# Where a third sum of weights is split, which columns it lands in, and when sums of weights are built in DRAM, in a one-core fp32 decoder block

## The chip, the cores and the metric

The kernel runs on one core of one Trainium2 chip. The metric is the device time of one execution in microseconds (us). A kernel is given by the median of several executions; one further execution is profiled, and the profile counts its times from the first instruction of that execution.

## What is computed

The reference is one decoder layer in float32 on 512 tokens of width 1024: an attention part (a sparse-attention mixer and an RWKV-7 mixer, merged by gates) and a gated MLP. The change touches the MLP and the building of its weights, and it moves transfers that stand beside the attention.

```python
def conv_ffn(h, w_up, conv_w, conv_b, w_down):        # h 512x1024, w_up 1024x5632, w_down 2816x1024
    u = h @ w_up
    up = jnp.pad(u, ((0, 0), (CONV_WIDTH - 1, 0), (0, 0)))
    c = conv_b + conv_w[0] * up[:, 0:s]
    for j in range(1, CONV_WIDTH):
        c = c + conv_w[j] * up[:, j:j + s]
    val, gate = jnp.split(c, 2, axis=-1)
    return (jax.nn.silu(gate) * val) @ w_down

for l in range(DEPTH):
    h = rmsnorm(x, attn_norm_g[l])
    proj = h @ w_in[l]
    ...
    o_a = nsa_mixer(...)
    o_b = rwkv7_mixer(...)
    merged = jax.nn.sigmoid(gate_a) * (o_a @ w_proj_a[l]) + jax.nn.sigmoid(gate_b) * (o_b @ w_proj_b[l])
    x = x + (merged @ w_out[l]).astype(x.dtype)
    h2 = rmsnorm(x, ffn_norm_g[l])
    x = x + conv_ffn(h2, w_up[l], conv_w[l], conv_b[l], w_down[l]).astype(x.dtype)
```

## The kernel before

**Products.** Every large product is made of three: an fp32 operand is split into a high part (`whi`, made by ScalarE, ACT, at L129) and a low part (`wlo`, the operand minus its high part, made by VectorE, DVE, at L132 or L367, or by GpSimd, POOL, at L367), and TensorE (PE) adds up high by high, low by high and high by low in PSUM. The PSUM tiles are named `ps_mm`, `ps_a` and `ps_b`. A matrix product of 128x512 takes about 0.23 us on PE and one of 128x256 about 0.12 us. The lines L123, L126, L129, L132 and L141 are those of helpers, so most of the work stands under these few lines, and one tells the instructions apart by their tiles.

**Stages.** First come the norm and the input projections (to 180 us), which build the inputs of the RWKV mixer; then the RWKV scan with the gate projections in its gaps (to 298); then the attention (298 to 392), in which scores are biased and their maxima taken by a custom instruction of DVE (L1274, `nm` is the negated maximum), exponentiated by ACT and scaled by DVE (L136, `P<-P,sm`), while the projection of the RWKV result (`ps_mm<-obT,whi`, weights `w_proj_b`) fills PE's gaps. The low parts of those eight weight tiles are subtracted by POOL (`wlo<-raw,whi 128x512`, L367). Then come the merge, the output projection and the second norm (to 470), the up-projection (470 to 694) and the down-projection (694 to 804).

**Up-projection.** The hidden columns are worked off in 22 pairs of a gate and a value column, numbered n. The pairs n = 5 to 20 are "quartered": the 512 tokens are two halves, the 1024 inputs two halves, and a scheme of seven products in place of eight is used (`quartered()`), 12 matmuls of 128x256 for each product. It needs the quarters B11, B12, B21 and B22 of the weights and three sums of them, `wsum3`, `wsum2` and `wsum4`. `QUARTER_TILES` lists which of these come together as one load: "top" (B11 and B12, whose sum POOL makes by a DMA that adds, L329), "third" (`wsum3`), "mid" (`wsum2`, B21) and "low" (`wsum4`, B22). "Mid" and "low" land in the rotating buffers `raw`; "top" and "third" land in columns of a tile `right` of 128 partitions by 11 columns of 512, which later holds the MLP's hidden values. `QUARTERED` gives, for each n, the first of the two columns of "top" and the one column of "third". All these loads are issued by `wload()` at L327 on the queue of SyncE (SP), one after the other, and one that has to wait holds up those behind it.

`first_quarters()` is called ahead of the pair and splits "top" and "third" into high and low parts; the split of "third" goes into two of the four buffers `split` (in the profile `s<-right`, 128x512 on ACT and then on DVE), taken in turn by even and odd n. `quartered()` then loads the rest, splits "mid" and "low", and makes the seven products; the fifth of them uses the split of "third" and so sets its buffer free. A scheduler places each instruction on its engine in the order in which its inputs and buffers are free in the scheduler's model, so the place of a line in the code is not the place of its instruction.

The finished hidden columns `right[:, i]` with i below 8 are copied to a DRAM tile `kept` by POOL (L1789), since their space is lent to weights, and fetched back by SP (L1760 for columns 0 to 3, L1790 for 4 to 7).

**Sums of weights in DRAM.** `wsum3`, `wsum2` and `wsum4` are built in DRAM ahead of the up-projection, in 48 pieces of 256 KB. Each piece is a copy issued by SP (L303) and then a DMA issued by POOL that adds the second summand (L300) and that has to wait for the copy. `pace()` hangs the pieces onto the ordinary weight loads, which it counts by `event`: `PACE` says how many pieces the SP queue takes behind a load, and POOL gets their additions at the next load.

**POOL's other work beside the attention.** `replicas()` (L1163 and L1165) copies the values into `Vr` by 16 DMAs and the compressed values into `sq` by 8, all issued by POOL. They stand in POOL's queue with the additions of L300 and the subtractions of L367.

**Down-projection.** It has a scheme of seven products too, with items (j, c, n) in a fixed list. `prepare()` makes ready an item two ahead of the product that PE runs: `difference()` builds a sum or difference of weights (into `raw`, `hA` or the tile `T2`, which the profile shows as `T`), and `parts()` splits it into `whi` and `wlo`. Loads of `w_down` are issued by `load_next()` (L1674). The order on DVE and ACT is that of the code here, not the scheduler's.

Of the kernel before, what the change touches and what calls it, by code (L numbers as in the profile page):

```python
# [32 lines left out]
NFH = NF // 2  # L33
# [50 lines left out]
def hybrid_block(ctx: ExitStack, tc: tile.TileContext, A: dict, out: bass.AP):  # L84
# [128 lines left out]
    def norm_tiles(pool_):  # L213
# [5 lines left out]

    order = [f for i in range(NFH) for f in (i, NFH + i)]  # L220

    QUARTERED = {n: ((0 if n % 2 == 0 else 6 if n < 11 else 2), (4 if n < 9 or 11 < n < 18 else 5 if n < 12 else 7))
                 for n in range(5, 21)}

    def weight_tiles():
        def cols(w, o, kt=KT, eng=v):
# [45 lines left out]

    BASE, SPAN = (3, NFH + 2), 1024
    WSUM = {j: [dp.tile([512, SPAN], F32, name=f"wsum{j}{h}") for h in range(2)] for j in (2, 3, 4)}
    QUARTER_TILES = {"top": ("B11", "B12"), "third": (3,), "mid": (2, "B21"), "low": (4, "B22")}

    def up_quarter(name, o, n):
        r, c = 512 * (name[1] == "2"), DFF * (name[2] == "1") + o
# [13 lines left out]
                    yield WSUM[j][h][r:r + 64], a[r:r + 64], b[r:r + 64]  # L292

    pieces, adding, event = sum_pieces(), [], itertools.count()
    PACE = {**{i: 1 for i in (*range(8, 26), *range(43, 49))}, **{i: 2 for i in range(49, 61)}}

    def pace(load):
        while adding:
# [1277 lines left out]
    def by_quarter(w):  # L1576
        return w.rearrange("p (q k) n -> p q k n", q=2)

    def first_quarters(top, third, mid, low):
        hi, lo = two_quarters()  # L1580
        halves(hi, lo, by_quarter(top))
        y = 2 * (next(turnsq) % 2)
        t3 = [split[y + j][:, :, NFH - 3].rearrange("p q (k n) -> p q k n", k=2) for j in range(2)]
        halves(*t3, by_quarter(third))
        return mid, low, (hi, lo), t3

    def quartered():
        mid, low, (h0, l0), (h3, l3) = ahead.pop(0)
        G, V, W = mmb(), mmb(), pa()[:, 0:256]
        act(V[:, 0:256], kc[:, 0:256], AF.Copy, scale=0.0)  # L1590
        U = hB[:, 256 * (NFH + 3):256 * (NFH + 5)]

        def product(o, hi, lo, j, start=False):
            his, los = ([w[:, k] if len(w.shape) == 3 else w[:, k // 2, k % 2] for k in range(4)] for w in (hi, lo))
            for k in range(4):
                mh, ml = moving(j, k)
                if start and k == 0:
                    te.matmul(o, lhsT=his[k], rhs=mh, start=True, stop=False, skip_group_check=True)
                else:
                    mm_on(o, his[k], mh, False)  # L1600
                mm_on(o, his[k], ml, False)
            for k in range(4):
                mm_on(o, los[k], moving(j, k)[0], False)

        for _ in range(len(QUARTER_TILES) - 1 if loads[0][3] == "quarters" else 1):
            wload()
        h1, l1 = two_quarters()
        with tc.high_priority():
            halves(h1[:, 0], l1[:, 0], mid[:, 0:4])
            halves(h1[:, 1], l1[:, 1], mid[:, 4:8])  # L1610
        product(W, h0[:, 0], l0[:, 0], -1, True)
        act(G[:, 0:256], W)
        product(V[:, 0:256], h0[:, 1], l0[:, 1], 0)
        act(V[:, 256:512], V[:, 0:256])
        h2, l2 = two_quarters()
        halves(h2, l2, by_quarter(low))
        product(W, h1[:, 0], l1[:, 0], 1)
        act(U[:, 0:256], W)
        product(G[:, 0:256], h1[:, 1], l1[:, 1], -2)
        wsplit()  # L1620
        product(W, h3, l3, 2)
        act(G[:, 256:512], W)
        act(U[:, 256:512], W)
        product(V[:, 0:256], h2[:, 1], l2[:, 1], 3)
        product(G[:, 256:512], h2[:, 0], l2[:, 0], -3)
        stt(V, V, -1.0, U, ALU.mult, ALU.subtract)
        return G, V
# [103 lines left out]
    def prepare():  # L1731
        k = len(ready)
        j, c, n = items[k]
        while len(summed) < min(k + 2, len(items)):
            difference()
        ready.append((parts(summed[k], n), operand(j, c, n)))

    def spare_half(c, n):
        halves_of(split[0][:, 0, c:c + n], split[0][:, 1, c:c + n], right[:, c:c + n, 0:256])
# [165 lines left out]
```

## Time and profile before

| | us |
|---|---|
| median of 3 runs | 807.81 |
| lowest and highest | 807.55 and 812.0 |
| the profiled execution, device time | 805.67 |
| its span from first to last instruction | 803.6 |
| PE busy | 790.4 (98%) |
| DVE busy | 635.9 (79%) |
| ACT busy | 485.2 (60%) |
| POOL busy | 122.0 (15%) |
| granted clock of PE | 1.000 |

A row of the timeline gives the start of an instruction in us from the first instruction, its duration, the engine, the line, the operation and its tiles, and in brackets how long the engine had been idle before it and what ended that idle time. The records of PE's matmuls overlap, so a matmul's duration there is longer than its share of PE's time; what a stall costs is read from the idle time in the brackets. A row of the waits gives an engine, the line that waited and the instruction waited for, then the total in us, how many times, and the longest. A row of the windows gives the stretch, its length and the busy time of each engine in it with the number of instructions.

### The profile page before, as it was taken

The page shows a single profiled execution, that of the slowest core. Times are in us where ns is not written, and L with a number is a line of the kernel's source. Part 1 is how long each engine was busy: PE and PEld are TensorE (multiplying, and loading weights), DVE is VectorE, ACT ScalarE, POOL GpSimd, SP SyncE. Part 2 cuts the span into 40 slices and gives each one's busy share as a digit, 9 for nine tenths or more (in the row PEclk, how much of TensorE's full clock was granted, in tenths as well). Part 3 has the DMA queues.
Part 4 walks back from the last instruction along what each step waited for, and adds up shares of the span by engine and source line. Part 5 has one row for each costly group of instructions (what it writes and reads, how often), then busy time and mean ns, then how long its engine had stood idle before and what let it go on. Part 6 is the DMA issues. An engine that isn't in the chain of part 4 may idle for free.

```text
span 803.6 us, 15422 instructions
## 1 busy us (share of the span) xinstructions
PE 790.4 (98%) x5829; PEld 672.5 (84%) x5829; DVE 635.9 (79%) x1227; ACT 485.2 (60%) x1003; POOL 122.0 (15%) x168
## 2 busy tenths in 40 slices
PE   8999999999999998999999999999989999999998
PEld 7777788987777887788788898899989999788886
DVE  6477869993665678889685489989989989998895
ACT  6766654563444567778344365678778778546452
POOL 6211013042000157123100000011101100000010
PEclk9999999999999999999999999999999999999999
DMA  7465557647576587455758333687878775676831
GB/s 240 115 157 144 144 114 178 170 110 202 147 127 150 124 211 168 93 126 122 175 162 275 127 95 116 189 233 212 216 197 225 214 206 167 206 245 213 271 106 53
DMA packets 149495, 135.53 MB, mean 169 GB/s; under 512 B 7862, under 2 KB 126573, under 8 KB 148397
## 3 DMA queue, kind: packets, MB, share of 16 engines
q1 hardware_dynamic: 139152, 110.10, 46.3%
q0 software_dynamic: 9216, 21.97, 15.6%
q10 hardware_dynamic: 1052, 2.48, 0.9%
q8 instruction: 46, 0.75, 0.4%
q14 instruction: 29, 0.23, 0.1%
HBM read 122.20 MB, written 31.65 MB: 191 GB/s over the span
## 4 chain that ended last, share of the span: by engine, by line
PE 86%; DVE 6%; DMA 3%; ACT 3%; issue 1%; POOL 0%; DVEq 0%; ACTq 0%; POOLq 0%; SPq 0%
PE ps_mm L123 51%; PE ps_mm L126 11%; PE ps_a L126 8%; PE ps_a L123 7%; PE ps_b L123 4%; PE ps_b L126 2%; DMA right<-wsum 2%; DVE wlo L132 1%; DMA kept<-right 1%; PE ps_b L1348 1%; ACT whi L129 1%; DVE P L136 1%; DMA pra<-in_rwkv_ln_b_dram 1%; PE ps_mm L1348 1%; DVE s L132 0%
## 5 line engine op out<-in xcount | busy, mean ns | idle before, releaser
L129 ACT ACTIVATE whi<-raw 128x512 fp32r<-128x512 f32 (+2 forms) x134 | 117.7, 891 | 101.0 <-PE ps_mm L123 57.9
L123 PE MATMUL ps_mm<-hh,whi 128*128 128x512 f32 (+1 forms) x368 | 142.9, 392 | 0.3 <-DVE hl L141 0.3
L123 PE MATMUL ps_mm<-hl,whi 128*128 128x512 f32 (+1 forms) x368 | 140.7, 386 | 0.0
L367 DVE TENSOR_TENSOR wlo<-raw,whi 128x1024 fp32r<-128x1024 f32 (+1 forms) x57 | 65.3, 1147 | 38.8 <-PE ps_mm L123 21.4
L123 PE MATMUL ps_mm<-hh,wlo 128*128 128x512 f32 (+1 forms) x368 | 88.8, 380 | 0.0
L123 PEld LDWEIGHTS ps_mm<-hh,whi 128*128 128x128 f32 x368 | 69.2, 188 | 17.1 <-issue 1.0
L123 PEld LDWEIGHTS ps_mm<-hl,whi 128*128 128x128 f32 x368 | 69.3, 188 | 12.9 <-issue 1.0
L123 PEld LDWEIGHTS ps_mm<-hh,wlo 128*128 128x128 f32 x368 | 67.1, 188 | 13.5
L300 POOL DMA_DIRECT2D wsum<-in_w_up_dram x48 | 39.2, 859 | 230.7 <-DMA wsum<-wsum 116.6
L132 DVE TENSOR_TENSOR wlo<-raw,whi 128x512 fp32r<-128x512 f32 (+1 forms) x64 | 58.5, 935 | 11.0 <-ACT whi L129 11.0
L141 DVE SCALAR_TENSOR_TENSOR right<-ps_mm,cw,right 128x511 f32<-128x511 f32 (+1 forms) x64 | 45.4, 741 | 1.2 <-ACT right L129 1.2
L129 ACT ACTIVATE P<-P,nm 128x512 f32<-128x512 f32 (+3 forms) x64 | 35.4, 554 | 13.5 <-DVE nm L1274 13.0
L329 POOL DMA_DIRECT2D right<-right x16 | 13.9, 870 | 188.7 <-DVE right L132 76.4
L126 PE MATMUL ps_mm<-hh,whi 128*128 128x256 f32 x128 | 32.2, 284 | 0.1
L126 PE MATMUL ps_mm<-hl,whi 128*128 128x256 f32 x128 | 32.1, 283 | 0.0
L1274 DVE CUSTOM_DVE_ANT_0 P<-ps_a,AB 128x512 f32<-128x512 f32 (+3 forms) x64 | 29.3, 482 | 1.6 <-PE ps_a L123 1.3
L367 POOL TENSOR_TENSOR wlo<-raw,whi 128x512 fp32r<-128x512 f32 (+3 forms) x13 | 22.1, 1701 | 40.0 <-PE ps_mm L123 22.4
L129 ACT ACTIVATE right<-ps_mm,cw 128x512 f32<-128x512 f32 x32 | 23.9, 769 | 4.2 <-DVE ps_mm L141 3.2
L129 ACT ACTIVATE QK<-ps_mm 128x64 f32<-128x64 f32 (+5 forms) x56 | 14.8, 309 | 17.9 <-PE ps_mm L123 13.7
L126 PEld LDWEIGHTS ps_mm<-hh,whi 128*128 128x128 f32 x128 | 24.6, 192 | 0.3 <-ACT ps_mm L129 0.3
L129 ACT ACTIVATE s<-right 128x512 fp32r<-128x512 f32 (+1 forms) x37 | 20.2, 552 | 7.4 <-DMA right<-wsum 6.7
L126 PEld LDWEIGHTS ps_mm<-hl,whi 128*128 128x128 f32 x128 | 24.6, 192 | 0.0
(489 smaller groups left out, 2118.3 us busy)
## 6 DMA issues: line engine op xcount, KB each, us to landing
raw<-in_w_in_dram SPq DMA_DIRECT2D x38, 512.0 KB, 4.6
wsum<-in_w_up_dram POOLq DMA_DIRECT2D x48, 256.0 KB, 4.6
raw<-in_w_down_dram SPq DMA_DIRECT2D x18, 512.0 KB, 4.1
wsum<-wsum SPq DMA_DIRECT2D x32, 256.0 KB, 4.3
right<-in_w_up_dram SPq DMA_DIRECT2D x32, 256.0 KB, 3.9
raw<-wsum SPq DMA_DIRECT2D x32, 256.0 KB, 3.1
raw<-in_w_up_dram SPq DMA_DIRECT2D x32, 256.0 KB, 3.9
raw<-in_w_up_dram SPq DMA_DIRECT2D x12, 512.0 KB, 4.8
```

The source lines that it names most:

```text
L123: te.matmul(o, lhsT=l, rhs=r, start=start, stop=stop)
L126: te.matmul(o, lhsT=l, rhs=r, start=False, stop=stop, skip_group_check=True)
L129: sc.activation(o, i, f, **kw)
L132: v.tensor_tensor(o, a, b, op=op)
L136: v.tensor_scalar(o, a, s1, None, op0=op0)
L141: v.scalar_tensor_tensor(o, a, s, b, op0=op0, op1=op1)
L300: nc.gpsimd.dma_start(o, x, accum_op=ALU.add)
L329: nc.gpsimd.dma_start(raw[:, 4:8], raw[:, 0:4], accum_op=ALU.add)
L367: low = eng.tensor_tensor(lo, raw, hi.bitcast(F32), op=ALU.subtract)
L1274: maxima.append(v.tensor_tensor_reduce(out=P[:, i], in0=o, in1=BT[:, h, 384 - 128 * qt:512], scale=-1.0, scalar=-NEG, op0=ALU.add, op1=ALU ...
L1348: te.transpose(pt[:, 128 * i:128 * i + 128], P[:, 4 * x + i, 128 * k:128 * k + 128], ident)
```

## The change

Three things are edited.

1. `QUARTER_TILES` lists "third" last. `first_quarters()` splits "top" alone; the split of "third" is written in `quartered()`, behind that of "low", and the load that follows it in the list is asked for there. The columns of "third" are now, for n = 5 to 20, 4, 5, 4, 5, 4, 5, 7, 6, 7, 4, 5, 4, 6, 7, 7, 7 (before: 4 for n = 5 to 8, 5 for 9 to 11, 4 for 12 to 17, 7 for 18 to 20).
2. `PACE` gives a second piece to the loads 11, 14, 17 and 20 and one to 37, 39 and 41; loads 49 to 52 get none (two before), 53 gets one, and 54 to 61 get two. The number of pieces is 48 as before.
3. `prepare()` splits the second item of the down-projection before it builds the difference of the third.

```diff
-    QUARTERED = {n: ((0 if n % 2 == 0 else 6 if n < 11 else 2), (4 if n < 9 or 11 < n < 18 else 5 if n < 12 else 7))
-                 for n in range(5, 21)}
+    QUARTERED = {n: ((0 if n % 2 == 0 else 6 if n < 11 else 2), c)
+                 for n, c in zip(range(5, 21), (4, 5, 4, 5, 4, 5, 7, 6, 7, 4, 5, 4, 6, 7, 7, 7))}
...
-    QUARTER_TILES = {"top": ("B11", "B12"), "third": (3,), "mid": (2, "B21"), "low": (4, "B22")}
+    QUARTER_TILES = {"top": ("B11", "B12"), "mid": (2, "B21"), "low": (4, "B22"), "third": (3,)}
...
-    PACE = {**{i: 1 for i in (*range(8, 26), *range(43, 49))}, **{i: 2 for i in range(49, 61)}}
+    PACE = {**{i: 1 for i in (*range(8, 26), 37, 39, 41, *range(43, 49), 53)}, **{i: 2 for i in (11, 14, 17, 20, *range(54, 62))}}
...
-    def first_quarters(top, third, mid, low):
+    def first_quarters(top, mid, low, third):
         hi, lo = two_quarters()
         halves(hi, lo, by_quarter(top))
-        y = 2 * (next(turnsq) % 2)
-        t3 = [split[y + j][:, :, NFH - 3].rearrange("p q (k n) -> p q k n", k=2) for j in range(2)]
-        halves(*t3, by_quarter(third))
-        return mid, low, (hi, lo), t3
+        return mid, low, third, (hi, lo)
 
     def quartered():
-        mid, low, (h0, l0), (h3, l3) = ahead.pop(0)
+        mid, low, third, (h0, l0) = ahead.pop(0)
...
-        for _ in range(len(QUARTER_TILES) - 1 if loads[0][3] == "quarters" else 1):
+        more = loads[0][3] == "quarters"
+        for _ in range(len(QUARTER_TILES) - 2 if more else 1):
             wload()
...
         halves(h2, l2, by_quarter(low))
+        y = 2 * (next(turnsq) % 2)
+        h3, l3 = (split[y + j][:, :, NFH - 3].rearrange("p q (k n) -> p q k n", k=2) for j in range(2))
+        halves(h3, l3, by_quarter(third))
+        if more:
+            wload()
         product(W, h1[:, 0], l1[:, 0], 1)
...
     def prepare():
         k = len(ready)
         j, c, n = items[k]
-        while len(summed) < min(k + 2, len(items)):
+        while k != 1 and len(summed) < min(k + 2, len(items)):
             difference()
         ready.append((parts(summed[k], n), operand(j, c, n)))
+        if k == 1:
+            difference()
```

How the instructions stand is shown at three places. The order on PE is the same in both kernels, row for row.

**ACT, late in pair n = 10.** The tile `right` here is the loaded sum, and `s_5290<-right 128x2x256` is the split of "third" for pair 12; `ps_mm<-ps_a` and `hB<-ps_a` empty PE's accumulators, and `s_5290<-hB` is work on hidden values. Before:

```order
L129 ACTIVATE s_5289<-hB 128x256
L129 ACTIVATE ps_mm<-ps_a 128x256
L129 ACTIVATE hB<-ps_a 128x256
L129 ACTIVATE s_5290<-hB 128x256
L129 ACTIVATE whi<-raw 128x512 x2
L129 ACTIVATE right<-ps_mm,cw 128x512 x2
L129 ACTIVATE ps_mm<-ps_a 128x256
L129 ACTIVATE s_5290<-right 128x2x256
L129 ACTIVATE whi<-raw 128x1024
```

Of the change:

```order
L129 ACTIVATE s_5289<-hB 128x256
L129 ACTIVATE s_5290<-right 128x2x256
L129 ACTIVATE ps_mm<-ps_a 128x256
L129 ACTIVATE hB<-ps_a 128x256
L129 ACTIVATE s_5290<-hB 128x256
L129 ACTIVATE whi<-raw 128x512 x2
L129 ACTIVATE right<-ps_mm,cw 128x512 x2
L129 ACTIVATE ps_mm<-ps_a 128x256
L129 ACTIVATE whi<-raw 128x1024
```

The split for pair 12 moved up by six rows, from pair 11 into pair 10; that for pair 6 moves up in the same way, and those for most other pairs keep their place, nearly two pairs ahead of their product.

**POOL, at the start of the attention.** `sq` and `Vr` are the copies of values, `wsum` the additions to the sums in DRAM, and the subtractions are those of `w_proj_b`. Before:

```order
L1165 DMA sq<-kc 32x64 x6
L367 TENSOR_TENSOR wlo<-raw,whi 128x512
L1163 DMA Vr<-vt 32x256 x12
L300 DMA wsum_103<-in_w_up_dram 64x1024 x2
L1163 DMA Vr<-vt 32x256
L367 TENSOR_TENSOR wlo<-raw,whi 128x512
L1163 DMA Vr<-vt 32x256 x3
L1165 DMA sq<-kc 32x64 x2
L300 DMA wsum_103<-in_w_up_dram 64x1024 x2
L300 DMA wsum_106<-in_w_up_dram 64x1024 x2
```

Of the change:

```order
L1165 DMA sq<-kc 32x64 x6
L367 TENSOR_TENSOR wlo<-raw,whi 128x512
L1163 DMA Vr<-vt 32x256 x16
L1165 DMA sq<-kc 32x64 x2
L367 TENSOR_TENSOR wlo<-raw,whi 128x512
L300 DMA wsum_103<-in_w_up_dram 64x1024
L367 TENSOR_TENSOR wlo<-raw,whi 128x512
L300 DMA wsum_106<-in_w_up_dram 64x1024 x2
```

The two additions between the copies are gone, and the last three `Vr` copies and two `sq` copies stand ahead of the second subtraction in place of behind it.

**DVE, where the down-projection begins.** `T_7886` is the tile `T2`; the first `wlo<-raw,whi` here is the low part of the second item, `wlo_7907<-T_7886,whi_7906` that of the third. Before:

```order
L132 TENSOR_TENSOR T_7886<-raw 128x1024
L141 SCALAR_TENSOR_TENSOR hA<-ps_mm,cw,hA 128x511
L132 TENSOR_TENSOR s_5291<-hB,s_5291 128x256
L141 SCALAR_TENSOR_TENSOR hA<-ps_mm,cw,hA 128x510
L132 TENSOR_TENSOR wlo<-raw,whi 128x1024
L132 TENSOR_TENSOR right<-hA 128x512
L132 TENSOR_TENSOR wlo_7907<-T_7886,whi_7906 128x1024
```

Of the change:

```order
L132 TENSOR_TENSOR wlo<-raw,whi 128x1024
L141 SCALAR_TENSOR_TENSOR hA<-ps_mm,cw,hA 128x511
L132 TENSOR_TENSOR s_5291<-hB,s_5291 128x256
L141 SCALAR_TENSOR_TENSOR hA<-ps_mm,cw,hA 128x510
L132 TENSOR_TENSOR T_7886<-raw 128x1024
L132 TENSOR_TENSOR right<-hA 128x512
L132 TENSOR_TENSOR hB<-right 128x256
L132 TENSOR_TENSOR hB<-hB,right 128x256
L132 TENSOR_TENSOR wlo_7907<-T_7886,whi_7906 128x1024
```

The low part of the second item and the difference for the third changed places, and the low part of the third item stands two short rows later.

## Prediction

> **What bounds the kernel now.** I read the share of busy time first, then PE's waits, then the timeline round each wait.
>
> ```profile
> PE 790.4 (98%) x5829; PEld 672.5 (84%) x5829; DVE 635.9 (79%) x1227; ACT 485.2 (60%) x1003; POOL 122.0 (15%) x168
> PE ps_a L123 <- DVE nm L1274: 2.3, 1, 2.3
> PE ps_a L126 <- ACT hB L129: 1.8, 2, 1.3
> PE ps_a L126 <- ACT ps_mm L129: 1.3, 1, 1.3
> ...
> PE ps_b L123 <- DVE wlo L132: 0.5, 1, 0.5
> ...
> PE ps_b L424 <- DMA pra<-in_rwkv_ln_b_dram: 0.2, 1, 0.2
> ```
>
> PE is busy for 790.4 of 803.6 us, so it is the bound, and the order of its work does not change. The change can win only what PE waits, 13.2 us in all, and of those rows it touches the surroundings of four: 2.3 (in the attention), 1.8 and 1.3 (up-projection), 0.5 (start of the down-projection). That is 5.9 us, less than 1% of the time. A loss has no such lid: a new wait on any engine ahead of PE would show at once.
>
> Since the records of PE overlap, the idle time in a row is a little less than what is lost: matmuls of 128x256 follow one another by 0.12 us while a record lasts 0.28 (four of them take 0.64 at 583.88, below), and those of 128x512 by some 0.23 with 0.39 (two take 0.61 at 701.35). A stall therefore costs its idle time and 0.16.
>
> **Change 1, "third" and its columns.** The two waits of the up-projection, with what stands ahead of them, on POOL, SP, ACT and PE in turn:
>
> ```profile
> 574.97 0.58 POOL L1789 DMA_DIRECT2D kept<-right  x1 [2.56 <-DVE right L132]
> 578.77 0.37 SPq L327 DMA_DIRECT2D right<-wsum  x1
> 583.12 0.63 ACT L129 ACTIVATE s<-right 128x512 fp32r<-128x512 f32 x1 [1.98 <-DMA right<-wsum]
> 591.30 0.63 ACT L129 ACTIVATE s<-right 128x512 fp32r<-128x512 f32 x1 [2.22 <-DMA right<-wsum]
> 583.88 0.64 PE L126 MATMUL ps_mm<-hh,wlo 128*128 128x256 f32 x4
> 585.84 0.75 PE L126 MATMUL ps_a<-s,s 128*128 128x256 f32 x4 [1.31 <-ACT hB L129]
> 594.64 0.74 PE L126 MATMUL ps_a<-s,whi 128*128 128x256 f32 x4 [1.35 <-ACT ps_mm L129]
> 648.66 0.50 PE L126 MATMUL ps_a<-s,s 128*128 128x256 f32 x2 [0.48 <-ACT hB L129]
> ACT s L129 <- DMA right<-wsum: 6.7, 5, 2.2
> ```
>
> The "third" for pair 12 goes into column 4, whose hidden values POOL has to copy away at 574.97; the load is issued at 578.77; ACT stands before the split from 581.14 to 583.12; the evictions behind it in its queue come late, and PE waits at 585.84. Pair 13 uses column 4 again, must wait for the split of pair 12, and the same follows at 591.30 and 594.64. So these two stalls, 1.31 + 0.16 + 1.35 + 0.16 = 2.98 us, hang on one column.
>
> With the change pair 12 uses column 6 and pair 13 column 7, both free long before. Column 4, copied away at 574.97, serves pair 14 only; the split of that stands after the fifth product of pair 12, so with pairs some 10.4 us apart (16 in 166 us) near 597. What is still late is another column at the same point of its life: column 5 for pair 15 and column 6 for pair 17, two and four pairs further on, loads near 600 and 621. From 578.77 to 583.12 issue, landing and waking of ACT took 4.3, so these can be split from about 604 and 625 on, and the splits stand near 607 and 628. They have some 2.7 us to spare. Pair 18 waits for column 7 in both kernels, and its 0.48 stays. The cost of the split itself, 0.63 on ACT and as much on DVE, is the same work for the same 16 pairs: though it is written behind the split of "low", the scheduler puts it as far ahead of its product as before, so there is nothing to price in the pair itself. For pair 6 it moves ahead of the first quartered pair and may wait for its load there; the dearest such wait so far held ACT for 2.22 and cost PE 1.5, the cheapest cost PE nothing (five waits in the row, three stalls). I take 0, with +1.5 as its other end. On SP "third" now stands behind "mid" and "low", which gives these an earlier place, and the order there is otherwise the same. I put change 1 at −3.0, ends −3.6 (the 0.48 and 0.16 go too) and 0.
>
> **Change 2, the pieces.** The first stall in the list stands in the attention:
>
> ```profile
> 306.57 1.28 DVE L136 TENSOR_SCALAR P<-P,sm 128x512 f32<-128x512 f32 x3
> 311.09 2.67 DVE L136 TENSOR_SCALAR P<-P,sm 128x512 f32<-128x512 f32 x1
> 314.41 0.50 PE L123 MATMUL ps_a<-KH,qst 128*128 128x512 f32 x1 [2.31 <-DVE nm L1274]
> 295.94 1.59 POOL L300 DMA_DIRECT2D wsum<-in_w_up_dram  x2 [6.73 <-DMA wsum<-wsum]
> 296.98 3.58 POOL L1165 DMA_DIRECT2D sq<-kc  x6
> 309.95 1.68 POOL L300 DMA_DIRECT2D wsum<-in_w_up_dram  x2
> 311.03 1.13 POOL L1163 DMA_DIRECT2D Vr<-vt  x1
> 311.58 1.88 POOL L367 TENSOR_TENSOR wlo<-raw,whi 128x512 fp32r<-128x512 f32 x1
> 312.80 2.10 POOL L1163 DMA_DIRECT2D Vr<-vt  x3
> 314.33 1.53 POOL L1165 DMA_DIRECT2D sq<-kc  x2
> 315.31 2.29 POOL L300 DMA_DIRECT2D wsum<-in_w_up_dram  x2
> L1163 POOL DMA_DIRECT2D Vr<-vt x16 | 9.4, 664 | 1.9 <-DMA Vr<-vt 1.2 <-DMA wsum<-in_w_up_dram 0.5 <-issue 0.2
> 372.76 1.30 POOL L367 TENSOR_TENSOR wlo<-raw,whi 128x512 fp32r<-128x512 f32 x1 [1.60 <-PE ps_mm L123]
> 373.02 1.07 DVE L132 TENSOR_TENSOR mx<-mx,gts 128x8 f32<-128x8 f32 x1
> ```
>
> Three scalings take 1.28, one takes 2.67 while a subtraction runs on POOL, and PE waits 2.31 for the maxima behind it. The same is seen at 373.02: a tiny operation (8 columns) lasts 1.07, to the end of POOL's 372.76 + 1.30. So it is the subtraction on POOL that stops DVE, not the additions, and the price is what is left of it. The change takes away the additions and so shifts when the subtraction starts. From 311.58 go the two additions at 295.94 (1.04 until the next row) and the two at 309.95 (1.08); ahead of it now come three `Vr` (312.80 to 314.33, 1.53) and two `sq` (to 315.31, 0.98): 311.97. If none of the 1.9 that the `Vr` copies waited comes back, 310.1. A start at 310.1 with 1.88 ends at 311.98, some 0.5 beyond the scaling's usual end of 311.52, and so costs about 0.6; a start at 311.5 costs the 2.3 again; from 311.6 on the scaling has passed. Averaged over the span that is some 1.1 lost of 2.47, so −1.4, ends −2.47 (missed) and 0 (met in full).
>
> The Trainium skill speaks against a row of copies issued by POOL: its page "SBUF — State Buffer", section "A bandwidth-pool intuition that's wrong (but worth ruling out)", has such a DMA at some 620 ns alone and 3100 ns beside a DVE copy. The row of six `sq` above went out 0.60 apart beside a busy DVE, so this case's trace does not bear it out. By the page even one such delay would, as an estimate, put the subtraction past 311.6 and make the term −2.47, if no other scaling is met.
>
> The pieces moved forward go where PE does not wait:
>
> ```profile
> 57.00:130.00 73.00, 73.00 (x462) 57.34 (x461) 57.46 (x78) 42.76 (x64) 12.92 (x14) 1.00 0.58 134
> 222.00:250.00 28.00, 28.00 (x348) 22.36 (x340) 16.44 (x47) 12.41 (x31) 1.59 (x2) 1.00 0.73 136
> ACT whi L129 <- PE ps_mm L123: 19.4, 7, 2.9
> 239.43 0.53 SPq L303 DMA_DIRECT2D wsum<-wsum  x1
> ```
>
> In both stretches PE is busy throughout (73.00 of 73.00, 28.00 of 28.00), and from 57 to 130 ACT waits 19.4 us for PE to set its split buffers free, not for loads. Seven more issues of 0.53 on SP are hidden behind that: 0. With the cover gone they would cost 7 x 0.53 = 3.7. The additions that go with them stand ahead of POOL's `KH` and `KL` copies; POOL is busy 1.59 of 28.00 in the second of these stretches, so I take 0 there too.
>
> **Change 3, the second low part first.**
>
> ```profile
> 694.42 1.23 DVE L132 TENSOR_TENSOR T<-raw 128x1024 f32<-128x1024 f32 x1 [0.95 <-PE ps_mm L123]
> 697.22 1.22 DVE L132 TENSOR_TENSOR wlo<-raw,whi 128x1024 fp32r<-128x1024 f32 x1
> 698.49 0.73 PE L123 MATMUL ps_b<-wlo,s 128*128 128x512 f32 x2 [0.47 <-DVE wlo L132]
> 701.35 0.61 PE L123 MATMUL ps_mm<-wlo,s 128*128 128x512 f32 x2
> 702.57 1.22 DVE L132 TENSOR_TENSOR wlo<-hA,whi 128x1024 fp32r<-128x1024 f32 x1
> 704.07 0.61 PE L123 MATMUL ps_a<-wlo,s 128*128 128x512 f32 x2
> 704.00:800.00 96.00, 95.95 (x429) 79.35 (x428) 81.40 (x93) 47.05 (x60) 2.23 (x4) 1.00 0.54 179
> ```
>
> The low part moves from 697.22 to 694.42 (`T` waited there for PE's last products of the up-projection, and they read the buffer of this low part too), so the 0.47 + 0.16 = 0.63 goes. The difference `T` moves to 697.22 and ends at 698.45; ACT takes 1.06 to split it (699.5), DVE 1.22 for its low part (700.8). PE wants that 0.63 earlier than 701.35, at 700.72: 0.1 late. Behind it on DVE three operations of 0.33, a sum and the next low part (1.13 each) end near 704.1, wanted at 704.07 − 0.63 + 0.1 = 703.5: 0.6 late. What is won is given back within two items, since DVE is full there: 0, ends −0.6 and +0.3. The fetch of the kept columns moves up by one load on SP; from 704 on PE is busy for 95.95 of 96.00, which hides it.
>
> **Sum.** −3.0 − 1.4 + 0 = −4.4. The profiled execution, 805.67 (span 803.6), would become 801.3. It lies 2.1 below the median, and I move the median by the same amount: 807.81 − 4.4 = **803.4 us**.
>
> **Rivals.** *The collision stays whole*: the subtraction starts near 311, for which the working of 311.97 speaks as well as against it; only −3.0 is left, 804.8. *It is missed whole*: −3.0 − 2.5, 802.3. *The wait only moves* to columns 5 and 6 (pairs 15 and 17), because their loads stand behind others on SP and the 2.7 us to spare are used up; for it speaks the traffic there, against it that the split stands later than the load by more than the 4.3 seen; the 3.0 comes back, 806.4. *Slower*: POOL's eight subtractions, all shifted in time, meet DVE's chain more often. Three of eight stretched an operation so far and one reached PE; each full hit costs 2.47. One more in addition to the present one leaves 0.5 of the gain; from two more it decides: 807.81 − 3.0 + 4.9 = 809.7. Against it: after the third subtraction their starts are set by PE setting buffers free, which does not move.
>
> **How the numbers follow.** Chances: the forecast 0.42, collision whole 0.20, missed 0.12, wait moves 0.13, slower 0.09, none of these 0.04. All ends at their best give −3.6 − 2.5 − 0.6 = −6.7, 801.1, and I allow some 0.7 below for the scatter of the runs; upward the range takes in the wait that moves and stops short of no change: 800.4 to 807.6. A measurement can tell about 1% (8.1 us) from no change. Faster by that would take more than all the stalls touched: 0.03. Slower by that would take three further full hits: 0.03. Within 1%: 0.94.
>
> **What would show it.** Right: ACT's waits for "third" fall from 6.7 in five to under 2; no stall of PE of over 1 us between 570 and 600; the stall before L1274's maxima is below 2.3; PE's wait for `wlo` at 698 is gone and smaller ones appear by 704. Wrong: stalls of PE near 608 or 628 (the wait moved); several scalings over 1.5 us (more hits); a wait of PE for a DMA beyond the 0.2 listed, in the first 250 us (the pieces).

## The result, and the profile after

The changed kernel takes 802.39 us (median of 5, 801.76 to 804.24), the kernel before 807.81; the ratio is 0.9934, with a 95% interval of 0.9911 to 0.9958. Forecast were 803.4 us, 800.4 to 807.6, and no change of over 1%.

The waits of PE in the profile after (engine, line and what it waited for, then us in total, times, longest):

```profile
PE ps_b L123 <- issue: 1.8, 1, 1.8
PE ps_b L123 <- DVE warm L156: 1.2, 1, 1.2
PE ps_a L126 <- ACT hB L129: 0.7, 1, 0.7
PE ps_mm L123 <- DVE oaT L132: 0.5, 1, 0.5
PE ps_mm L123 <- DVE wlo L132: 0.4, 1, 0.4
...
PE ps_a L123 <- DVE wlo L132: 0.3, 1, 0.3
```

The wait of 2.3 for DVE's maxima and the two of 1.3 in the up-projection are gone. In place of the 0.5 at the start of the down-projection stand two, 0.4 and 0.3. New is the first row, 1.8 with no cause that the profile shows. The profiled execution happens to be the longest of the five, 804.24 us (span 802.2); what it holds and the others do not is told below.

**Up-projection.** The split of "third" on ACT from pair 12 on, the loads of columns 5 and 6 on SP, and PE's one stall:

```profile
576.40 0.62 ACT L129 ACTIVATE s<-right 128x512 fp32r<-128x512 f32 x1
586.57 0.61 ACT L129 ACTIVATE s<-right 128x512 fp32r<-128x512 f32 x1
...
606.73 0.61 ACT L129 ACTIVATE s<-right 128x512 fp32r<-128x512 f32 x1
...
626.89 0.62 ACT L129 ACTIVATE s<-right 128x512 fp32r<-128x512 f32 x1
643.93 0.63 ACT L129 ACTIVATE s<-right 128x512 fp32r<-128x512 f32 x1 [1.40 <-DMA right<-wsum]
599.93 0.92 SPq L327 DMA_DIRECT2D right<-wsum  x2
621.26 0.37 SPq L327 DMA_DIRECT2D right<-wsum  x1
```

and, of the waits between 517 and 683, the one that had been 6.7:

```profile
ACT s L129 <- DMA right<-wsum: 1.4, 1, 1.4
```

ACT no longer stands before a split until pair 18; its waits for "third" fell from 6.7 us in five to 1.4 in one.

**Attention.** POOL's queue and DVE's scaling:

```profile
295.60 2.97 POOL L1165 DMA_DIRECT2D sq<-kc  x6 [7.44 <-PE ps_b L123]
298.59 1.30 POOL L367 TENSOR_TENSOR wlo<-raw,whi 128x512 fp32r<-128x512 f32 x1
299.82 8.14 POOL L1163 DMA_DIRECT2D Vr<-vt  x16
307.96 0.99 POOL L1165 DMA_DIRECT2D sq<-kc  x2
308.96 1.28 POOL L367 TENSOR_TENSOR wlo<-raw,whi 128x512 fp32r<-128x512 f32 x1
...
311.11 0.49 DVE L136 TENSOR_SCALAR P<-P,sm 128x512 f32<-128x512 f32 x1
```

The 16 copies go out without a gap, the subtraction ends at 310.24, and the scaling begins at 311.11 and takes 0.49 in place of 2.67.

**Down-projection.** DVE's operations that matter, and PE:

```profile
692.48 1.23 DVE L132 TENSOR_TENSOR wlo<-raw,whi 128x1024 fp32r<-128x1024 f32 x1 [1.02 <-PE ps_mm L123]
695.27 1.21 DVE L132 TENSOR_TENSOR T<-raw 128x1024 f32<-128x1024 f32 x1
...
697.58 0.42 DVE L132 TENSOR_TENSOR hB<-hB,right 128x256 f32<-128x256 f32 x1
697.92 1.22 DVE L132 TENSOR_TENSOR wlo<-T,whi 128x1024 fp32r<-128x1024 f32 x1
...
701.20 1.22 DVE L132 TENSOR_TENSOR wlo<-hA,whi 128x1024 fp32r<-128x1024 f32 x1
695.83 0.61 PE L123 MATMUL ps_b<-wlo,s 128*128 128x512 f32 x2
699.20 0.74 PE L123 MATMUL ps_mm<-wlo,s 128*128 128x512 f32 x2 [0.35 <-DVE wlo L132]
702.47 0.74 PE L123 MATMUL ps_a<-wlo,s 128*128 128x512 f32 x2 [0.25 <-DVE wlo L132]
```

PE does not wait at 695.83, where it waited 0.47 before, and does so at 699.20 and 702.47.

**Where the time went.** PE does the same matmuls in the same order in all these kernels, so the nth of one profile can be set beside the nth of another, and the steps in the difference of their starts tell place by place what was won and lost. Against the profile of before (us):

| kernel | attention, at 314 | small matmuls, 385 to 400 | up-projection, 517 to 660 | down-projection, 694 to 745 | elsewhere | all |
|---|---|---|---|---|---|---|
| the change | −2.2 | +3.4 | −3.3 | +0.6 | 0.0 | −1.4 |
| the change again (e12_change_again) | −2.2 | +0.5 | −3.7 | +0.6 | 0.0 | −4.7 |

In its first profile the change wins 4.9 us at the places it touches and loses 3.4 between 385 and 400 to a pause of PE and a slower clock behind it, which the profile of before lacks altogether. In its second the pause costs 0.5.

### The profile page after: what moved, and what is told of

Same layout as the page of the kernel before. It is cut to its first block, busy times and chain, and to the rows that moved or that the text cites. A ratio compares the mean times of both kernels' runs of the same rounds, so it can differ in the third digit from the quotient of the medians.

```text
span 802.2 us, 15423 instructions
## 1 busy us (share of the span) xinstructions
PE 792.6 (99%) x5829; PEld 674.2 (84%) x5829; DVE 633.8 (79%) x1227; ACT 484.2 (60%) x1003; POOL 121.5 (15%) x168
## 4 chain that ended last, share of the span: by engine, by line
PE 90%; DVE 4%; DMA 2%; ACT 2%; issue 1%; POOL 0%; DVEq 0%; POOLq 0%; ACTq 0%; SPq 0%
PE ps_mm L123 51%; PE ps_mm L126 13%; PE ps_a L126 9%; PE ps_a L123 7%; PE ps_b L123 4%; PE ps_b L126 2%; DVE wlo L132 1%; PE ps_b L1348 1%; DMA pra<-in_rwkv_ln_b_dram 1%; PE ps_mm L1348 1%; ACT whi L129 1%; DVE P L1274 0%; DMA kept<-right 0%; DMA right<-wsum 0%; POOL pra L170 0%
## 5 line engine op out<-in xcount | busy, mean ns | idle before, releaser
L1274 DVE CUSTOM_DVE_ANT_0 P<-ps_a,AB 128x512 f32<-128x512 f32 (+3 forms) x64 | 29.3, 481 | 1.8 <-PE ps_a L123 1.5
L129 ACT ACTIVATE whi<-T 128x1024 fp32r<-128x1024 f32 (+1 forms) x12 | 11.9, 991 | 17.7 <-DVE T L132 10.0
```

The costliest lines, as they stand in the source:

```text
L129: sc.activation(o, i, f, **kw)
L1274: maxima.append(v.tensor_tensor_reduce(out=P[:, i], in0=o, in1=BT[:, h, 384 - 128 * qt:512], scale=-1.0, scalar=-NEG, op0=ALU.add, op1=ALU ...
```

## The experiments

Each kernel has one profile; those of more than one run are timed beside the kernel before. The last columns are the steps as above.

| kernel | median us | ratio to before, 95% | attention | 385 to 400 | up-projection | down-projection | all |
|---|---|---|---|---|---|---|---|
| e1_third | 803.44 | 0.9957, 0.9938 to 0.9977 | −0.5 | +1.5 | −3.1 | 0.0 | −2.2 |
| e2_pieces | 805.93 | 0.9981, 0.9962 to 1.0 | −2.2 | +0.9 | −0.8 | 0.0 | −2.1 |
| e3_low_first | 807.54 | 1.0008, 0.9988 to 1.0029 | −1.5 | +3.1 | −0.4 | +0.6 | +1.7 |
| e4_without_low | 801.15 | 0.9923, 0.9898 to 0.9948 | −2.2 | +0.8 | −3.2 | 0.0 | −4.7 |
| e5_columns | 804.26 | 0.9955, 0.9932 to 0.9978 | −1.0 | +1.0 | −3.8 | 0.0 | −3.9 |
| e6_c18_6 | 800.9 | 0.9925, 0.9899 to 0.9952 | −2.2 | +0.5 | −4.3 | 0.0 | −6.0 |
| e7_halves | 804.33 (one run) | | −1.1 | +0.1 | −0.8 | 0.0 | −1.4 |
| e8_pieces_early | 803.43 | 0.9958, 0.9938 to 0.9979 | −2.2 | +0.2 | −3.4 | 0.0 | −1.9 |
| e9_clear | 803.45 | 0.9934, 0.9916 to 0.9951 | −2.2 | 0.0 | −4.3 | 0.0 | −2.2 |
| e10_traffic | 802.85 (one run) | | −2.2 | +0.2 | −4.3 | 0.0 | −2.8 |
| e11_sub_dve | 804.08 (one run) | | −2.2 | +0.2 | −0.9 | 0.0 | −1.3 |
| e12_change_again | 802.46 | 0.9929, 0.9911 to 0.9946 | −2.2 | +0.5 | −3.7 | +0.6 | −4.7 |

The median of the kernel before was 806.85 beside the first four, 808.06 beside the next four and 808.53 beside the last.

In four kernels the four places do not add up to the last column: some 3.5 us lie elsewhere in e8_pieces_early, 4.1 in e9_clear, 3.4 in e10_traffic and 1.6 in e11_sub_dve. Most of it is told below; up to 0.6 of it falls before 57 us, and the cause of that is open.

### The three edits one by one

The first kernel has the first edit alone, the second the new `PACE` alone, the third the new `prepare()` alone; the fourth is the change without the last:

```diff
-        while k != 1 and len(summed) < min(k + 2, len(items)):
+        while len(summed) < min(k + 2, len(items)):
             difference()
         ready.append((parts(summed[k], n), operand(j, c, n)))
-        if k == 1:
-            difference()
```

> The kernel before with edit 1 alone (order of the weight tiles, split of the third sum, its columns). Theory, three edits that act apart: the stalls of PE near 526, 585 and 594 go (-0.4, -1.6, -1.6), the wait of pair 18 stays (+0.2), the stall of 2.3 in the attention stays whole and the start of the down-projection is as before: 3.3 us less in the alignment of PE's work, about 804.5. Rival, the pieces are what freed the columns' loads: then ACT's waits for the third sum stay near 6.7 us and the time near 807.8.

> The kernel before with edit 2 alone (when the pieces of the sums are built). Theory: POOL's second subtraction ends before the scaling at 311, which then takes 0.49 in place of 2.67; PE gains 2.2 there and nothing anywhere else: about 805.6. Rival, the additions themselves and not the subtraction stop DVE: they are moved to other places and some other scaling is stretched by over 1 us, gain below 1. Rival, the denser pieces late in the attention cost PE a pause near 390 of some 2 us as in the profile of the change: then no gain in the runs, 807 to 808.

> The kernel before with edit 3 alone (second low part before the difference for the third item). Theory: PE's wait of 0.6 at 698 goes, two others of 0.6 and 0.5 come behind it, and from 694 on the kernel is 0.4 to 0.6 slower: 808.2 to 808.4. Rival, the two waits in the profile of the change come from loads that arrive later there: then edit 3 alone gains 0.6, 807.2.

> The change without edit 3. Theory: 0.4 to 0.6 faster than the change from 694 on, the rest alike: some 801.9, and faster than both kernels. Rival, as for edit 3 alone: 0.6 slower than the change.

By place the edits act apart, as expected: the up-projection's gain comes with the first (−3.1), the attention's with the second (−2.2), the down-projection's loss with the third (+0.6). The medians do not test this so finely: the first alone wins 3.4 us, the second alone 0.9, both together 5.7, and each interval is 1.6 to 2.0 wide to either side.

The kernels without the new columns win something in the up-projection too (e2_pieces −0.8, e3_low_first −0.4, e7_halves −0.8, e11_sub_dve −0.9). In these four the stall near 585 is 0.6 to 1.0 shorter than in the profile of before, while the one near 594 is within 0.3 of it. So the stall near 585 differs from execution to execution, and the profile of before holds a large one. Only in the kernels with the new columns are both gone.

PE's two new waits in the kernel with the third edit alone, where no load was moved:

```profile
702.32 0.73 PE L123 MATMUL ps_mm<-wlo,s 128*128 128x512 f32 x2 [0.37 <-DVE wlo L132]
705.60 0.74 PE L123 MATMUL ps_a<-wlo,s 128*128 128x512 f32 x2 [0.26 <-DVE wlo L132]
```

They are 0.37 and 0.26, as 0.35 and 0.25 in the change: it is the order on DVE that makes them, not a late load. Timed alone, 0.6 us cannot be told from nothing (0.9988 to 1.0029); the trace tells it. Without this edit the fourth kernel is at 0.9923.

Another thing did not come as expected. The stall of the attention was to stay whole in the first and third kernels, whose instructions there are those of before, and it was 0.5 and 1.5 shorter. So its size, too, differs from execution to execution, and the profile of before holds a large one. In the first kernel it was not the scaling that was held but a tiny operation on 4 columns ahead of it:

```profile
310.85 1.81 DVE L132 TENSOR_TENSOR sm<-sm,gts 128x4 f32<-128x4 f32 x1
...
310.73 1.89 POOL L367 TENSOR_TENSOR wlo<-raw,whi 128x512 fp32r<-128x512 f32 x1
```

Its usual 0.17 became 1.81, and it ended with POOL's subtraction (312.66 and 312.62).

### Which part of the first edit

```diff
-    QUARTERED = {n: ((0 if n % 2 == 0 else 6 if n < 11 else 2), (4 if n < 9 or 11 < n < 18 else 5 if n < 12 else 7))
-                 for n in range(5, 21)}
+    QUARTERED = {n: ((0 if n % 2 == 0 else 6 if n < 11 else 2), c)
+                 for n, c in zip(range(5, 21), (4, 5, 4, 5, 4, 5, 7, 6, 7, 4, 5, 4, 6, 7, 7, 7))}
```

> The kernel before with nothing but the new list of columns for the third sum; the order of the weight tiles and the place of the split in the code stay as before. Theory: the columns are all there is to edit 1; the stalls near 585 and 594 go (about -3.1 in the alignment of PE's work from 517 to 660), as with the whole of edit 1, about 803.5 where the kernel before has 806.85. Rival, the order of the loads (third last) is what lets the others come earlier: then one of the two stalls stays, over 805.

With nothing but the list of columns both stalls go (−3.8 in this profile), and the time is 0.9955 of before, as with the whole edit (0.9957). The order of the loads and the place of the split in the code, most of the edit's lines, move nothing that these runs can tell. The scheduler put the splits at the same places: on ACT those for pairs 8 to 17 stand 1.07 to 1.08 us ahead of those of e1_third, which is the lead that PE has there.

The same rule applied to the pair whose wait was left:

```diff
-(4, 5, 4, 5, 4, 5, 7, 6, 7, 4, 5, 4, 6, 7, 7, 7)
+(4, 5, 4, 5, 4, 5, 7, 6, 7, 4, 5, 4, 6, 6, 7, 7)
```

> The change without edit 3, and pair 18 takes its third sum from column 6 instead of 7. Theory: what a pair waits for is the copy of a column's hidden values to DRAM; column 6 is free since pair 17's split, so ACT's wait of 1.4 near 644 and PE's of 0.7 to 0.9 near 647 go, and pairs 19 and 20 (column 7) get theirs early too: 0.9 less than without this, about 800.2. Rival, column 6 is written by pair 18's own values and its load has to wait for or holds up something there: no gain, or PE waits elsewhere between 625 and 670.

In its profile ACT has no wait for "third" left; the splits for pairs 17, 18 and 19 stand at

```profile
623.85 0.62 ACT L129 ACTIVATE s<-right 128x512 fp32r<-128x512 f32 x1
633.84 0.61 ACT L129 ACTIVATE s<-right 128x512 fp32r<-128x512 f32 x1
643.87 0.63 ACT L129 ACTIVATE s<-right 128x512 fp32r<-128x512 f32 x1 [0.38 <-PE ps_a L126]
```

and PE runs through the whole up-projection without a stall. The profile gains the 0.7 that this stall cost before and the 0.4 by which it had grown in e4_without_low; the medians, 800.9 here and 801.15 without it, cannot tell so little. It is the version with the shortest profile, 6.0 below that of before.

### What holds DVE in the attention

The kernel before with each of POOL's subtractions cut in two:

```diff
-            low = eng.tensor_tensor(lo, raw, hi.bitcast(F32), op=ALU.subtract)
+            if eng is nc.gpsimd and (kt, n) == (4, 128):
+                for i in (0, 2):
+                    low = eng.tensor_tensor(lo[:, i:i + 2], raw[:, i:i + 2], hi[:, i:i + 2].bitcast(F32), op=ALU.subtract)
+            else:
+                low = eng.tensor_tensor(lo, raw, hi.bitcast(F32), op=ALU.subtract)
```

> The kernel before with POOL's eight subtractions for w_proj_b each done as two instructions of 128x256. Theory, DVE is held by one POOL instruction until it ends: the longest stretched operation of DVE in the attention falls from 1.8 to 2.7 to under 1.5, and PE's stall near 314 from 2.3 to under 1.2. Rival, DVE and POOL slow each other for as long as both have work: the stretch stays at 1.8 or more. Second rival, the additions issued by POOL just before hold DVE: no change either, and the stretched operation ends before the subtractions start.

```profile
311.64 1.26 DVE L136 TENSOR_SCALAR P<-P,sm 128x512 f32<-128x512 f32 x1
...
311.89 2.26 POOL L369 TENSOR_TENSOR wlo<-raw,whi 128x256 fp32r<-128x256 f32 x2
...
313.56 0.50 PE L123 MATMUL ps_a<-KH,qst 128*128 128x512 f32 x1 [1.19 <-DVE nm L1278]
```

The scaling is held for 0.8 us instead of 2.2 and is done long before POOL's pair of instructions (312.90 and 314.15). Taken alone this decides little, since whole subtractions gave stalls of 0.8 to 2.3 here. Near 371 the comparison is clean. There, in all twelve profiles with whole subtractions on POOL, an operation of DVE on 8 columns takes 1.03 to 1.07 in place of 0.17 and ends 0.02 to 0.03 after the subtraction. With the halves:

```profile
372.12 0.51 DVE L132 TENSOR_TENSOR mx<-mx,gts 128x8 f32<-128x8 f32 x1
371.86 1.44 POOL L369 TENSOR_TENSOR wlo<-raw,whi 128x256 fp32r<-128x256 f32 x2 [1.51 <-PE ps_mm L123]
...
372.57 0.73 POOL L369 TENSOR_TENSOR wlo<-raw,whi 128x256 fp32r<-128x256 f32 x1
```

The last row is the second half by itself. The operation takes 0.51 and ends at 372.63, as the second half takes over from the first. And the kernel before with the subtractions on DVE, POOL's DMAs left as they are:

```diff
-            yield cols(A["w_proj_b"][0], 128 * m, NH2, eng=pool_)
+            yield cols(A["w_proj_b"][0], 128 * m, NH2)
```

> The kernel before with the eight subtractions for w_proj_b on DVE instead of POOL; POOL's additions and copies stay. Theory, the subtractions on POOL hold DVE: no operation of DVE between 298 and 392 is over 0.6 us above the usual length of its shape, PE's stall near 314 is under 0.4 from that cause, and DVE's own eight more subtractions (0.7 each) may cost PE a few tenths elsewhere. Rival, POOL's issuing of DMAs holds DVE: an operation near 311 is still stretched by over 0.6.

```profile
311.44 0.17 DVE L132 TENSOR_TENSOR sm<-sm,gts 128x4 f32<-128x4 f32 x1
311.64 0.49 DVE L136 TENSOR_SCALAR P<-P,sm 128x512 f32<-128x512 f32 x1
```

No operation of DVE in the attention is stretched, though POOL issues the same copies and additions. So a subtraction on POOL holds an operation of DVE until it ends. That POOL's DMAs never do is not shown, since two profiles have a stretched operation that is over before any subtraction starts. The first is that of e3_low_first:

```profile
310.77 0.79 DVE L132 TENSOR_TENSOR sm<-sm,gts 128x4 f32<-128x4 f32 x1
...
311.89 2.14 POOL L367 TENSOR_TENSOR wlo<-raw,whi 128x512 fp32r<-128x512 f32 x1
```

The second is that of the halves (0.45 from 311.15, where 0.17 is usual). In both POOL's rows at that time are additions and a copy. In e11_sub_dve no operation beside an addition is over 0.02 longer than usual, so what held these two is open. POOL's rows overlap one another there and may be too rough to tell. Moved to DVE the subtractions cost 1.0 us elsewhere in the attention (at 366), so this is no better place for them.

The Trainium skill has this in "SBUF — State Buffer", section "Who interferes with whom": DVE and GpSimd share a pair of ports, whoever issues first holds it for its whole instruction, and a DVE instruction with two inputs in SBUF contends with a GpSimd instruction that reads SBUF. The two rows of the first kernel (0.17 grown to 1.81) and the rows near 371 agree with it. In the profile of before and in that of the halves the stretched scaling starts 0.49 and 0.25 ahead of the subtraction by the records, which that rule alone does not give. The same section exempts DVE instructions with at most one SBUF input outside the two-port modes, and the custom instruction of L1274, one of whose two inputs is in PSUM, is indeed not stretched in any of these profiles.

### When the pieces are built

> The change without edit 3, with most pieces of the sums moved to the start: two at each of the loads 8 to 25, single ones after, none from load 56 on, so no such traffic beside PE's small matmuls near 388. Theory: PE's pause near 389 to 391, seen in all profiles but that of before, is the wait for a 16 KB fetch of instructions (queue 8), which takes 1.0 to 1.8 us in that traffic; with little traffic it takes 1.0 or less and the pause is under 0.8 us; the early pieces hide; some 0.5 faster than the change without edit 3, 800.7. Rival, the pause has nothing to do with the traffic and stays at 0.7 to 1.9. Second rival: two pieces for each load delay the loads, PE waits for them between 57 and 130, and the kernel is slower by over 3 us.

```diff
-    PACE = {**{i: 1 for i in (*range(8, 26), 37, 39, 41, *range(43, 49), 53)}, **{i: 2 for i in (11, 14, 17, 20, *range(54, 62))}}
+    PACE = {**{i: 2 for i in range(8, 26)}, **{i: 1 for i in (37, 39, 41, *range(43, 49), 53, 54, 55)}}
```

The pause near 390 is down to 0.2, but PE loses 2.9 us between 130 and 298, in two waits:

```profile
PE ps_a L123 <- POOL QK L778: 1.4, 1, 1.4
PE ps_b L123 <- issue: 1.3, 1, 1.3
```

Neither is the delayed load that the second rival named. POOL has more additions ahead of a small setting of constants (`QK`), and PE waits for that. The other stands beside matmuls of 32x32 that follow one another by some 0.01 us:

```profile
174.15 0.21 PE L123 MATMUL ps_b<-AB,sg 32*32 32x32 f32 x1 [1.25 <-issue]
```

It ends 1.29 us after a 16 KB transfer of instructions has landed (171.88 + 0.98), as the pauses near 390 do (below). So the first stretch has room for the change's four extra pieces and not for 18.

> The change without edit 3, column 6 for pair 18, and the four pieces of loads 59 and 60 moved behind loads 62 and 63, so that no sums are built while PE runs its small matmuls near 387. Theory: in ten profiles PE resumed 1.2 to 1.4 us after the 16 KB fetch of instructions had landed, and the fetch was late by what other transfers were in its way; with these out of the way it starts some 1.8 after the small matmuls begin, takes about 1.0, and the pause is under 0.2. Alignment of PE's work against before: -6.4 in all, some 800.4. Rival, the pause is set by something else and stays at 0.3 to 1.8.

```diff
-(11, 14, 17, 20, *range(54, 62))
+(11, 14, 17, 20, *range(54, 59), 61, 62, 63)
```

No pause of over 0.1, as expected. But the time is 803.45, not 800.4: the pieces behind the later loads hold up the weights of the next two projections, and between 392 and 470 PE waits for splits that wait for loads.

```profile
PE ps_mm L123 <- ACT whi L129: 1.9, 1, 1.9
PE ps_mm L123 <- DVE ta L141: 0.8, 1, 0.8
```

and ACT's from 400 to 420:

```profile
ACT whi L129 <- DMA raw<-in_w_proj_a_dram: 6.3, 1, 6.3
...
ACT whi L129 <- DMA raw<-in_w_out_dram: 2.3, 1, 2.3
```

What was won at 390 (0.5) was given back eight times over (3.9). The kernel with added traffic below has the same pieces there and loses 2.9 at the same place.

### The pause

In all profiles a transfer of 16 KB on queue 8, which carries instructions, lands shortly before the matmul at which PE pauses, if it does. Worked out from the records of transfers and of PE (us; the small matmuls are those of `Vr`, 32x64, in two groups of 128; within a group they follow one another by some 0.01; the pause is always at the same matmul, in the second group):

```
                      small matmuls begin   transfer begins   takes   PE goes on after it landed   step at that place
before                387.10                +1.86             1.06    1.25                         0
the change            384.90                +3.79             0.95    1.31                         +1.9
e1_third              386.48                +3.41             0.95    1.32                         +1.5
e2_pieces             384.80                +1.97             1.76    1.39                         +0.9
e4_without_low        384.75                +1.76             1.79    1.38                         +0.8
e7_halves             386.08                +1.75             1.34    1.32                         +0.2
e9_clear              385.12                +1.86             1.06    1.33                         +0.1
e10_traffic           385.42                +1.84             1.25    1.29                         +0.2
```

The matmul after the pause starts 1.2 to 1.4 us after the landing in these eight, and 1.2 to 1.5 after it in all fourteen profiles. Where the transfer starts some 1.8 us after the small matmuls begin and takes 1.1, PE goes on without a pause; where it starts or lands late, PE stands. That PE waits for these instructions is read from the times, and e8_pieces_early has the same 1.29 at another place; no run moved the transfer on purpose. To test whether traffic makes it late, copies that nothing uses were put there:

```diff
+        for i in range(4 if at in (59, 60) else 0):
+            r = 64 * i + 256 * (at - 59)
+            more = nc.sync.dma_start(extra[r:r + 64], up_quarter("B11", 0, SPAN)[r:r + 64])
```

> As the kernel with the traffic cleared, with eight copies of 256 KB into an unused DRAM tile put behind loads 59 and 60, so that there is more traffic than in any kernel so far while PE runs its small matmuls. Theory: the fetch of instructions starts later than 3 us after the small matmuls begin, or takes over 1.6, and PE pauses for 1.0 to 2.5 us until 1.3 after it has landed. Rival, the pause does not follow the traffic: under 0.4, as with the traffic cleared.

The theory fails in this form: eight copies of 256 KB more, and the transfer started at +1.84, took 1.25, and the pause cost 0.2. What makes it late remains open. The three kernels without additions issued by POOL at that time (e8_pieces_early, e9_clear, e10_traffic) have at most 0.2, the others from 0 to 1.9 (in e11_sub_dve 1.0, behind 0.8 won just ahead of it); that would fit the additions, but one profile each is no proof.

> The change itself once more, beside the version with the traffic cleared. Theory: the attention and the up-projection are as in its first profile (-2.2 and -3.3 against before), the down-projection's start again +0.4 to +0.6; only the pause near 390 and the slower clock behind it differ, 0.3 to 1.9 and 0 to 1.6: 801.5 to 803, and 1 to 2 us above the version with the traffic cleared. Rival, the pause of the first profile was part of the change: again over 1.5 with the slower clock.

In the second profile of the change PE pauses for 0.4 where it paused for 1.8, and no slower clock follows; the span is 798.9 instead of 802.2. So the large pause was the lot of that one execution, and not part of the change. By the medians this kernel (802.46) and the one with the traffic cleared (803.45) stand within each other's intervals, 0.9911 to 0.9946 and 0.9916 to 0.9951; the expected lead of the latter did not come.

## Why the prediction was right

**The bound.** It put PE's waits at 13.2 us, 5.9 of them in reach, and a change of over 1% out of reach. The gain of 5.4 us lies within that.

**Change 1, −3.0.** Measured −3.3 and −3.7 in the two profiles of the change, −3.1 alone. The two stalls are −1.6 each in every kernel with the new columns; the rest is −0.4 near 526, which the sum did not have, and the scatter of pair 18's wait. Against the mean of the five profiles with the old columns (0, −0.8, −0.4, −0.8, −0.9) the gain is 3.5 − 0.6 = 2.9. The cause was one column in the wrong place of its life, as argued, and the list of columns alone shows it. The times worked out for the new late columns came true: loads near 600 and 621 (599.93, 621.26), splits near 607 and 628 (606.73, 626.89), no wait there. The rival by which the wait only moves is out. Pair 18's wait, said to stay at 0.48, is 0.74 in one profile.

**Change 2, −1.4.** Here the mechanism was right and the size was off. The subtraction was to start between 310.1 and 312.0; it started at 308.96. Three things make the difference. The waits between the `Vr` copies went (16 went out in 8.14), 1.8 us for the twelve that stood ahead of it. The row of `sq` began 1.4 earlier, where 1.0 was worked out. And POOL's first subtraction, which the sum did not have, kept the next row waiting for 1.23 (298.59 to 299.82), where it had been 2.08 before (300.00 to 302.08):

```profile
300.00 1.88 POOL L367 TENSOR_TENSOR wlo<-raw,whi 128x512 fp32r<-128x512 f32 x1
```

The second took 1.28, not the 1.88 with which its end was worked out. So the collision was missed whole, −2.2, in all eight profiles of kernels without additions between the copies: the rival given 0.12 came true. The claim that the subtraction stops DVE was argued from one small operation; the rows near 371 and the subtractions on DVE show it. That the additions play no part was argued too, and is not shown. The row of six `sq` that was set against a delayed issue was no real test, since DVE ran no copy beside it; in the change the 16 `Vr` copies went out 0.51 apart with DVE busy for 7.80 of 8.14. What was not seen is that the 2.31 of the profile was a large draw: in three kernels with the same instructions there (e1_third, e5_columns, e3_low_first) it was 0.5, 1.0 and 1.5 less. Against the mean of the four the gain is 2.2 − (0 + 0.5 + 1.0 + 1.5) / 4 = 1.4.

**The pieces moved forward, 0.** Shown: PE is as busy from 57 to 130 as before (73.00 of 73.00 in the profile after), and the table has nothing elsewhere. The cover is not without end, as e8_pieces_early shows; what ends it is POOL's queue, which was not priced.

**Change 3, 0.** Measured +0.6. The step "0.1 late" for the third item's low part was mis-sized: PE lost 0.64 there. Some 0.3 of that is a short operation which stands on DVE between ACT's split and the low part and begins as the split ends (697.58). At the low part after it PE lost another 0.53 (forecast 0.6). The first low part won 0.75 (forecast 0.63). The +0.6 lies 0.3 beyond the end given, +0.3.

**Sum and median.** −4.4 forecast, −5.4 measured; by place −2.2 − 3.5 + 0.6 = −5.1, without the pause near 390, which no term had (+0.5 and +3.4 with its clock, and 0 to 3.1 in the kernels with the old pieces). That the sum came so close is in part luck: the stalls of the profile of before near 314 and 585 were large draws, and against the means of the profiles the terms are −1.4, −2.9 and +0.6, −3.7 in all. Which places make up the rest of the median's gain is not known. The constant 2.1 between profile and median did not hold, since the change's first profile lies 1.9 above its median and its second 1.5 below. The chances named for slower and faster by 1% were small for the right reason: nothing in reach was that large.

## What to carry to other kernels

Where one transfer waits for a buffer, ask which event frees it and give the late user another buffer: a list of 16 numbers did all that these runs can tell of what the reordered code around it did. When PE's order is the same in two kernels, set their matmuls side by side and read the steps; that tells 0.3 us by place, where the medians' intervals are 2 us wide to either side. And take a second profile before a stall of 2 us is called a property of the kernel: collisions between engines and pauses are drawn anew in each execution.

## What the runs showed of the hardware that was not expected

By the times in the table of the pause, PE can run out of instructions. Where it works off matmuls of 32x64 that follow one another by some 0.01 us, and a fetch of 16 KB starts 2 us later than in the profile of before (+3.79 against +1.86), it stands:

```profile
390.95 0.27 PE L123 MATMUL ps_b<-PTs,Vr 32*64 32x64 f32 x2 [1.77 <-issue]
```

The window behind it, with the clock granted to PE, the share of the DMA engines and GB/s as its last three columns:

```profile
393.00:396.00 3.00, 3.00 (x8) 2.33 (x8) 1.67 (x4) 0.48 (x1) 1.59 (x2) 0.50 0.27 23
```

In the profile of the change it stood for 1.77, and afterwards the clock granted to it was 0.50 from 393 to 396, which cost another 1.5 us by 400; in the profile of e3_low_first, with a pause of 1.46, the same followed, and after a pause of 1.39 (e1_third) it did not. A wait "<- issue" on PE near many small matmuls is to be looked up among the transfers of instructions.
